# Decay broadcasts on the GpSimd queue, and the first FFN block's input products inside the last SSD step

## The chip, the cores and the metric

The kernel runs on one core of one Trainium2 chip. The metric is the device time of one execution in microseconds (us). The engines are called as in the profile: PE is TensorE (PEld its weight loads), DVE is VectorE, ACT is ScalarE, POOL is GpSimd, SP is SyncE. SPq and POOLq are the DMA issues of SP and POOL.

## The reference

One inference step of a two-layer trunk over 1024 prompt tokens and 8 samples of 8 tokens, width 1024, in float32. Layer 0 has an SSD mixer, layer 1 an S5 mixer, and each mixer is followed by a SwiGLU FFN:

```python
for i in range(DEPTH):
    sh1, sc1, g1, sh2, sc2, g2 = split(silu_c @ ada_w[i] + ada_b[i], 6)
    h = rms(x) * (1 + sc1) + sh1
    out = ssd_mixer(h) if i % 2 == 0 else s5_mixer(h)
    x = x + g1 * out
    h = rms(x) * (1 + sc2) + sh2
    x = x + g2 * swiglu(h)
```

The SSD mixer projects h to z, x, B, C and dt, runs a short convolution and silu over x, B and C, and then a chunked scan. Within a chunk of 128 tokens, with a_cs the running sum of dt * A for each head:

```python
decay = exp(where(causal, a_cs[l] - a_cs[s], -inf))
y_diag = einsum(C B^T * decay, x * dt)
y_off = einsum(C, state_in) * exp(a_cs)
```

The result is gated with silu(z), normed over each of 8 groups, and projected back.

## The kernel before

The tokens are in two halves of the class Half: 512 prompt tokens, and 512 with the 64 sample tokens behind them. Features lie on partitions and tokens along the free dimension. Every weight and activation of a dense product is split into two float32r parts, and a product takes three matmuls (`mm3`, lines 134 to 136). A weight comes in by one 512 KB load from SP (`weight_cols`, `weight_block`, lines 122 and 129), is cast on ScalarE (line 114) and its remainder is taken on VectorE (line 115). Loads of ada_w (line 327) are slipped in ahead of weight loads as long as any are left. There are three buffers for loaded weights and two for split ones.

`mixers` runs 16 steps, one for each half and each of the 8 groups. A step consists of `ssd` for its group, `z_part`, the `out_proj` that is due (groups in the parts 0, 1-2, 3-4, 5-6, 7), `group_out`, and `begin` for the next step, which holds the input products and convolutions. At the last group of a half `begin` also makes the z products and the norm factors of the other half. A 17th round of the loop held only the last `out_proj`.

In `ssd` a chunk needs two things that are spread over partitions out of DRAM. `decays` (line 554) loads ab, the running sums of four heads, to every partition, 128 x 4 x 128 values, 256 KB; ScalarE makes exp(a[l] - a[s]) of it (lines 556 and 558), VectorE masks it (line 598), and PE takes it at line 605 (py). ab has three buffers. Line 579 loads ea, exp(a_cs), in two transfers for a chunk, 64 KB each, into two buffers. In the second half a fifth chunk holds the samples; `sample_state` loads and stores their states from SP.

The group norm of `group_out` takes the squares' sum over 256 features (`rstd_cols`, small products gp and gb, and Newton steps on VectorE) and gives pairs yh, yl, four buffers each, to `out_proj`. `ffn_norm` (through `norm`, `modulated`, lines 214, 220, 240, 241) gives the pairs h of the FFN. `ffn_in` makes some tiles of the hidden features, two weight matrices for each; `ffns` runs `ffn_in` one block ahead of `out_proj`. During FFN tiles `side` takes one or two steps of `s5_matrices`, the preparation of the S5 layer, whose POOL transfers are lines 995, 1007, 1023, 1035 and 1039; the S5 layer's own input transfers are lines 1079 and 1082.

What sets the order: the program is traced in the order of the code, which gives each instruction its priority, and a planner with a cost model then lays out each engine's queue and the buffers' use at compile time. An engine, and a DMA queue, works its list in that order; waits are semaphores.

Of the kernel before, what the change touches and what calls it, by code (L numbers as in the profile page):

```python
# [6 lines left out]
F32 = mybir.dt.float32  # L7
# [28 lines left out]
class Half:  # L36
    """A part of the tokens: 512 of the prompt, the second one with the samples behind them."""
# [13 lines left out]
class Trunk:  # L51
    def __init__(self, tc, ctx, ins, outs):
# [4 lines left out]
        self.pn = None  # L57
# [25 lines left out]
    def mixc(self, shape, name):  # L83
        """A constant of the mixers alone."""
        return self.cm.tile(shape, F32, name=name, tag=name)
# [39 lines left out]
    def weight_block(self, w, r0, nk, c0, n):  # L125
        """Rows r0.. (nk tiles) and columns c0.. of a weight matrix."""
# [23 lines left out]
    def add_resid(self, hf, li, piece, ft, o, n, src):  # L150
        """x += gate * src for the columns o.. of a half."""
# [13 lines left out]
    def rstd_cols(self, tiles, hf, scale, eps, name):  # L165
        """1/sqrt(mean of squares over the partitions of all tiles + eps): a column for each 128 tokens."""
# [8 lines left out]
        # by token on partitions: 1/sqrt from a first guess out of the exponent, in three Newton steps  # L175
# [18 lines left out]
    def rstd(self, tiles, hf, scale, eps, name):  # L194
        """The same along the tokens, on every partition."""
# [12 lines left out]
    def modulated(self, hf, li, sh, sc, ft, r, out, pview, sview):  # L208
        """out = x * r * (1 + scale) + shift; the views arrange the columns of out."""
# [21 lines left out]
    def norm(self, hf, li, sh, sc, r=None):  # L231
        """The modulated norm of x as float32r pairs, a pair for each 128 features."""
# [13 lines left out]
    def constants(self):  # L246
# [6 lines left out]
        # causal[s, l] = 1 where l >= s  # L253
# [3 lines left out]
        # bmask[s, b] = 1 where token s is of sample b  # L257
# [7 lines left out]
        # two[j, p] = 1 where p // 64 == j  # L265
# [5 lines left out]
    def flip(self, src, rows, name, alloc=None):  # L271
        """Rows of 128 values (a DRAM view [rows, 128]) as columns: [128, rows]."""
# [9 lines left out]
    def load_x(self, hf):  # L282
        """A function for each 128 tokens of a half."""
# [39 lines left out]
    def ada(self, li, cb, j):  # L323
        """Rows j * 256.. of silu(c) @ ada_w for 512 columns, 128 columns in each quarter of the partitions."""
# [16 lines left out]
    def ada_out(self):  # L341
        """The last such product + ada_b (+ 1 for the scales), as columns of mod."""
# [14 lines left out]
    def ssd_setup(self):  # L357
# [19 lines left out]
        # sblk[s, l] = 1 where s and l are tokens of one sample; pick[s, b] = 1 for the first token of b  # L377
# [5 lines left out]
        # conv states of the samples, [128, tile, (b, k)]  # L383
# [6 lines left out]
    def conv_states(self):  # L390
        """A function for each quarter of the samples' conv states."""
# [15 lines left out]
    def dt_part(self, hf, h):  # L407
        """dt, its running sums and decays, by head on partitions and by token on partitions."""
# [26 lines left out]
        # softplus: max(v, 0) + log(1 + e^-|v|), the logarithm by the series of atanh  # L435
# [15 lines left out]
        # running sums over the tokens of a chunk, and the whole sums  # L451
# [26 lines left out]
        # by head on partitions, to spread over the partitions from DRAM  # L478
# [13 lines left out]
    def conv_tile(self, hf, h, c0, t, pad):  # L492
        """A tile of x, B or C: in_proj, conv and silu. t: its index in the conv's channels."""
# [56 lines left out]
    def decays(self, col, m, g, acs):  # L550
        """exp(a[l] - a[s]) for the four heads of a group, [s, head, l]; 1 where l < s."""
        nc = self.nc
        ab = self.mp.tile([P, 4, P], F32, name=self.nm("ab"), tag="ab", bufs=3)
        nc.sync.dma_start(ab[:m, :, :m], self.d_acs[None, 4 * g : 4 * g + 4, col : col + m].broadcast_to([m, 4, m]))
# [6 lines left out]
    def ssd(self, hf, g, tok, C, B, xt, y):  # L561
# [7 lines left out]
        for c in range(nck + (1 if hf.samples else 0)):  # L569
# [6 lines left out]
            if not first:  # L576
                ea = self.mp.tile([P, 2, P], F32, name=self.nm("ea"), tag="ea")
                for j in range(2):
                    nc.sync.dma_start(
# [59 lines left out]
    def sample_state(self, g, C, xe, bt, yv, ea):  # L639
        """The samples' part of y that comes from their states, and their new states."""  # L640
# [40 lines left out]

    def group_out(self, hf, g, y, xt, zs):
        """The gated group norm of y, as pairs for out_proj."""
# [7 lines left out]
        for t in range(2):  # L691
            u = y[:, t]
            V.scalar_tensor_tensor(u, u, self.nw[:, 2 * g + t : 2 * g + t + 1], r, MUL, MUL)
            yh = self.mp.tile([P, hf.n], F32R, name=self.nm("yh"), tag="yh", bufs=4)
            yl = self.mp.tile([P, hf.n], F32R, name=self.nm("yl"), tag="yl", bufs=4)
# [5 lines left out]
    def mixers(self):  # L701
        """The SSD layer over both halves."""
# [17 lines left out]
        for i in range(len(steps) + 1):  # L720
            if i < len(steps):
                hf, g = steps[i]
                C, B, xt = nxt
                y = self.mp.tile([P, 2, hf.n], F32, name=self.nm("y"), tag="y", bufs=1)
                self.ssd(hf, g, tok, C, B, xt, y)
                if g < GR - 1:
                    zs = self.z_part(hf, h, g)
                else:
                    zs = z
                    if hf.i == 0:  # L730
                        h = self.norm(self.halves[1], 0, 0, 1, r)
                    else:
                        self.ahead = self.ffn_norm(0, self.halves[0], r)
            if due:
                self.out_proj(due[0], 0, 2, self.ssd_out_w[0], 2 * due[1] * P, due[2])
                due = None
            if i < len(steps):
                done += self.group_out(hf, g, y, xt, zs)
                for p in parts:
                    if p[-1] == g:  # L740
                        due = (hf, p[0], done)
                        done = []
            if i + 1 < len(steps):
                nxt = begin(i + 1)

    def out_proj(self, hf, li, piece, w, r0, yp):
        """x += gate * (pairs yp) @ (rows r0.. of w)."""
# [35 lines left out]
    def ffn_in(self, li, hf, c0, nt):  # L783
        """Some tiles of the hidden features, as pairs."""
        nc = self.nc
        if c0 == 0:
# [5 lines left out]
        for j in range(nt):  # L792
# [3 lines left out]
            u = self.fp.tile([P, hf.n], F32, name=self.nm("fu"), tag="fu", bufs=2)  # L796
# [5 lines left out]
            yh = self.fp.tile([P, hf.n], F32R, name=self.nm("fh"), tag="fh")  # L802
            yl = self.fp.tile([P, hf.n], F32R, name=self.nm("fl"), tag="fl")
# [9 lines left out]
    def ffns(self, steps, more=(), last=()):  # L813
        """FFN steps; more: what else to emit behind a step; last: what to emit ahead of the last part's product."""
# [13 lines left out]
    def cmul(self, ore, oim, ar, ai, br, bi, t1, t2):  # L828
        """(ore, oim) = a * b, complex; the outputs are not among the inputs."""
# [8 lines left out]
    def s5_matrices(self):  # L838
# [7 lines left out]
        with self.tc.tile_pool(name="s5pre", bufs=1) as pp, self.tc.tile_pool(name="s5big", bufs=1) as bp:  # L846
# [15 lines left out]
            # ang - 2 pi round(ang / 2 pi), the multiple of 2 pi in three parts  # L862
# [8 lines left out]
            # sine and cosine of half the angle by their series  # L871
# [11 lines left out]
            # sin = 2 a b, cos = 1 - 2 a a  # L883
# [7 lines left out]
            # q = (a - 1) / lambda  # L891
# [14 lines left out]
            # to [(j n), q]  # L906
# [6 lines left out]
            # powers 0..8 of a  # L913
# [19 lines left out]
            # Bbar [(j n), q, i]  # L933
# [9 lines left out]
            # C_re and -C_im as [(j n), q, i]  # L943
# [14 lines left out]
            # the same with the two groups of a pair in columns of their own  # L958
# [9 lines left out]
            # D in the last 16 of 128 rows, for the diagonal of lag 0  # L968
# [14 lines left out]
            def powers(q0):  # L983
# [9 lines left out]
                # Or = Re(C a^(l+1)), Oi = -Im(C a^(l+1))  # L993
# [348 lines left out]
```

## Time and profile before

| | us |
|---|---|
| median of 3 runs | 3255.96 |
| lowest and highest run | 3253.51, 3258.48 |
| span of the profiled execution | 3254.6 |
| PE busy in it | 3094.3 |
| DVE, ACT, POOL busy in it | 1903.7, 1222.6, 175.5 |

The span runs from the first to the last instruction of one execution on the chip; the profile gives no further time around it. The mixers end near 1250 us, the first FFN of layer 0 follows. The page names the engine's busy time, the queries of the trace give single instructions with the idle time ahead of them and what ended it. "PEclk" is the clock granted to PE as a share of full speed.

### The profile page before, as it was taken

The page shows a single profiled execution, that of the slowest core. Times are in us where ns is not written, and L with a number is a line of the kernel's source. Part 1 is how long each engine was busy: PE and PEld are TensorE (multiplying, and loading weights), DVE is VectorE, ACT ScalarE, POOL GpSimd, SP SyncE. Part 2 cuts the span into 40 slices and gives each one's busy share as a digit, 9 for nine tenths or more (in the row PEclk, how much of TensorE's full clock was granted, in tenths as well). Part 3 has the DMA queues.
Part 4 walks back from the last instruction along what each step waited for, and adds up shares of the span by engine and source line. Part 5 has one row for each costly group of instructions (what it writes and reads, how often), then busy time and mean ns, then how long its engine had stood idle before and what let it go on. Part 6 is the DMA issues. An engine that isn't in the chain of part 4 may idle for free.

```text
span 3254.6 us, 52528 instructions
## 1 busy us (share of the span) xinstructions
PE 3094.3 (95%) x20800; PEld 2719.9 (84%) x20800; DVE 1903.7 (58%) x4269; ACT 1222.6 (38%) x2183; POOL 175.5 (5%) x360
## 2 busy tenths in 40 slices
PE   7999999999999998999999989999998999999998
PEld 5777777788888986777899989988877879999998
DVE  4776668666677677865464572446448243544344
ACT  4553445444444444222342224235332442422222
POOL 0010000111011100102001000000000000000000
PEclk7999999999999998999999999999999999999999
DMA  6445554545434333444433436333452642223221
GB/s 224 141 134 179 154 163 123 156 138 146 120 95 124 102 90 84 122 129 131 126 96 123 154 104 195 99 96 99 135 166 80 207 130 78 80 84 110 78 89 65
DMA packets 552057, 402.74 MB, mean 124 GB/s; under 512 B 50323, under 2 KB 501291, under 8 KB 551796
## 3 DMA queue, kind: packets, MB, share of 16 engines
q1 hardware_dynamic: 545156, 377.36, 39.1%
q0 software_dynamic: 6656, 22.03, 2.3%
q8 instruction: 164, 2.69, 0.3%
q14 instruction: 81, 0.66, 0.1%
HBM read 363.70 MB, written 46.89 MB: 126 GB/s over the span
## 4 chain that ended last, share of the span: by engine, by line
PE 70%; DVE 10%; DMA 9%; issue 7%; ACT 3%; POOL 1%; SPq 0%; ACTq 0%; POOLq 0%; DVEq 0%
PE mm L134 15%; PE mm L136 15%; PE mm L135 15%; PE mo L134 5%; PE mo L136 5%; PE mo L135 5%; DMA ab<-d_acs 4%; DMA om<-d_o 2%; DVE wl L115 2%; DMA aw<-in_ada_w_dram 2%; PE ada L334 1%; PE py L605 1%; PE y L1156 1%; PE sn L674 1%; DVE sc L1115 1%
## 5 line engine op out<-in xcount | busy, mean ns | idle before, releaser
L136 PE MATMUL mm<-hh,wl 128*128 128x288 f32 (+3 forms) x3672 | 1213.1, 330 | 15.9 <-DVE wl L115 15.8
L134 PE MATMUL mm<-hh,wh 128*128 128x288 f32 (+3 forms) x3672 | 1218.8, 332 | 7.4 <-ACT wh L114 2.4
L135 PE MATMUL mm<-hl,wh 128*128 128x288 f32 (+3 forms) x3672 | 1211.3, 330 | 0.0
L114 ACT CAST wh<-wr 128x1024 fp32r<-128x1024 f32 (+1 forms) x426 | 445.6, 1047 | 1140.9 <-PE mm L135 762.2
L136 PEld LDWEIGHTS mm<-hh,wl 128*128 128x128 f32 (+1 forms) x3672 | 693.7, 189 | 71.1 <-DVE wl L115 22.2
L134 PEld LDWEIGHTS mm<-hh,wh 128*128 128x128 f32 (+1 forms) x3672 | 693.7, 189 | 69.6 <-issue 10.0
L115 DVE TENSOR_TENSOR wl<-wr,wh 128x1024 fp32r<-128x1024 f32 (+1 forms) x426 | 519.1, 1219 | 386.9 <-ACT wh L114 374.9
L135 PEld LDWEIGHTS mm<-hl,wh 128*128 128x128 f32 (+1 forms) x3672 | 693.9, 189 | 53.0 <-issue 5.3
L134 PE MATMUL mo<-fh,wh 128*128 128x288 f32 (+1 forms) x1056 | 351.2, 333 | 16.2 <-DVE x L156 10.2
L156 DVE SCALAR_TENSOR_TENSOR x<-mo,mod,x 128x288 f32<-128x288 f32 (+2 forms) x408 | 231.7, 570 | 210.7 <-PE mo L136 210.1
L136 PE MATMUL mo<-fh,wl 128*128 128x288 f32 (+1 forms) x1056 | 348.8, 330 | 4.0 <-DVE wl L115 4.0
L135 PE MATMUL mo<-fl,wh 128*128 128x288 f32 (+1 forms) x1056 | 347.8, 329 | 0.0
L801 DVE TENSOR_TENSOR fu<-fu,mm 128x288 f32<-128x288 f32 (+1 forms) x132 | 70.0, 531 | 312.7 <-PE mm L136 311.3
L134 PEld LDWEIGHTS mo<-fh,wh 128*128 128x128 f32 x1056 | 200.3, 190 | 35.5 <-issue 10.9
L136 PEld LDWEIGHTS mo<-fh,wl 128*128 128x128 f32 x1056 | 200.2, 190 | 19.6 <-DVE wl L115 4.9
L135 PEld LDWEIGHTS mo<-fl,wh 128*128 128x128 f32 x1056 | 200.5, 190 | 14.0
L522 DVE SCALAR_TENSOR_TENSOR xbc<-pre,cw,xbc 128x512 f32<-128x512 f32 (+1 forms) x288 | 161.6, 592 | 11.5 <-ACT xbc L508 9.3
L556 ACT ACTIVATE ab<-ab,tacs 128x128 f32<-128x128 f32 (+1 forms) x288 | 97.0, 390 | 133.0 <-DMA ab<-d_acs 115.3
L134 PE MATMUL mo<-yh,wh 128*128 128x288 f32 (+1 forms) x384 | 133.5, 348 | 9.5 <-DVE rs L160 4.9
L135 PE MATMUL mo<-yl,wh 128*128 128x288 f32 (+1 forms) x384 | 129.8, 338 | 0.0
L136 PE MATMUL mo<-yh,wl 128*128 128x288 f32 (+1 forms) x384 | 128.9, 337 | 0.3 <-DVE wl L115 0.3
L134 PEld LDWEIGHTS mo<-yh,wh 128*128 128x128 f32 x384 | 74.2, 194 | 22.9 <-issue 8.7
(368 smaller groups left out, 3232.8 us busy)
## 6 DMA issues: line engine op xcount, KB each, us to landing
wr<-in_ffn_w_in_dram SPq DMA_DIRECT2D x176, 512.0 KB
aw<-in_ada_w_dram SPq DMA_DIRECT2D x96, 512.0 KB
wr<-in_ssd_in_w_dram SPq DMA_DIRECT2D x96, 512.0 KB
wr<-in_ffn_w_out_dram SPq DMA_DIRECT2D x88, 512.0 KB
ab<-d_acs SPq DMA_DIRECT2D x64, 256.0 KB
wr<-in_ssd_out_w_dram SPq DMA_DIRECT2D x32, 512.0 KB
wr<-in_s_glu_w_dram SPq DMA_DIRECT2D x32, 512.0 KB
st<-in_state_ssm_dram SPq DMA_DIRECT2D x32, 256.0 KB
```

Source lines behind the costliest of these rows:

```text
L114: nc.scalar.copy(hi, raw)
L115: nc.vector.tensor_tensor(lo, raw, hi.bitcast(F32), SUB)
L134: mm(ps, wh, hh, start=first, stop=False)
L135: mm(ps, wh, hl, start=False, stop=False)
L136: self.last_mm = mm(ps, wl, hh, start=False, stop=last)
L156: nc.vector.scalar_tensor_tensor(self.xs(hf, ft, o, npr), src[:, :npr], mod[:, t, 0:1], self.xs(hf, ft, o, npr), MUL, ADD)
L334: nc.tensor.matmul(self.ada_ps[q * 32 : (q + 1) * 32], self.ct[:, 2 * j + k, :], w[:, k, q * P : (q + 1) * P], start=j + k == 0, stop=j == ...
L522: V.scalar_tensor_tensor(dst, src(k), w(k), dst, MUL, ADD)
L556: nc.scalar.activation(ab[:m, r, :m], ab[:m, r, :m], AF.Relu, bias=acs[:m, 4 * g + r : 4 * g + r + 1], scale=-1.0)
L605: nc.tensor.matmul(py[q * HD : (q + 1) * HD, (r // 2) * P : (r // 2) * P + m], xd[:m, r * HD : (r + 1) * HD], w[:m, r, :m], start=True, st ...
L674: nc.tensor.matmul(pn[q], xe[r, t * P : (t + 1) * P], bb[r].rearrange("p b k -> p (b k)"), start=True, stop=True)
L801: nc.vector.tensor_tensor(u[:, o : o + n], u[:, o : o + n], pu[:, :n], MUL)
```

## The change

`decays` and the ea loads are issued by POOL in place of SP. `mixers` loses its 17th round: in the last step `ssd_finish` (the output of the convolution states) and the FFN norm of the first half are traced ahead of `ssd`, the first FFN block's `ffn_in` (two tiles) between the due `out_proj` and `group_out`, and the last `out_proj` and the block's own `out_proj` follow the loop. For that block the hidden pairs come out of the buffers of yh and yl, and the product u out of the pool for temporaries. `ffns` starts with the second block. Comments and docstrings are gone, which moves no instruction.

```diff
@@ decays, ssd
-        nc.sync.dma_start(ab[:m, :, :m], self.d_acs[None, 4 * g : 4 * g + 4, col : col + m].broadcast_to([m, 4, m]))
+        nc.gpsimd.dma_start(ab[:m, :, :m], self.d_acs[None, 4 * g : 4 * g + 4, col : col + m].broadcast_to([m, 4, m]))
...
-                    nc.sync.dma_start(
+                    nc.gpsimd.dma_start(
                         ea[j * HD : (j + 1) * HD, :, :m],
@@ group_out
+    def ypair(self, hf):
+        return tuple(self.mp.tile([P, hf.n], F32R, name=self.nm(t), tag=t, bufs=4) for t in ("yh", "yl"))
@@ mixers
-        for i in range(len(steps) + 1):
...
+        ffn = self.ffn_steps(0, self.halves[0])[0]
+        for i in range(len(steps)):
+            hf, g = steps[i]
+            end = i + 1 == len(steps)
+            C, B, xt = nxt
+            y = self.mp.tile([P, 2, hf.n], F32, name=self.nm("y"), tag="y", bufs=1)
+            if end:
+                self.ssd_finish()
+                self.ahead = self.ffn_norm(0, self.halves[0], r)
+            self.ssd(hf, g, tok, C, B, xt, y)
+            if g < GR - 1:
+                zs = self.z_part(hf, h, g)
+            else:
+                zs = z
+                if not end:
+                    h = self.norm(self.halves[1], 0, 0, 1, r)
             if due:
                 self.out_proj(due[0], 0, 2, self.ssd_out_w[0], 2 * due[1] * P, due[2])
                 due = None
...
+            if end:
+                hid = self.ffn_in(*ffn)
+            done += self.group_out(hf, g, y, xt, zs)
...
+            if not end:
                 nxt = begin(i + 1)
+        self.out_proj(due[0], 0, 2, self.ssd_out_w[0], 2 * due[1] * P, due[2])
+        self.out_proj(ffn[1], 0, 5, self.ffn_w_out[0], 0, hid)
@@ ffn_in
+        early = self.fp is None
...
+            u = (self.th([P, hf.n], "fu") if early else
+                 self.fp.tile([P, hf.n], F32, name=self.nm("fu"), tag="fu", bufs=2))
...
+            if early:
+                yh, yl = self.ypair(hf)
@@ front, run
             self.mixers()
-            self.ssd_finish()
...
-            fa, fb = self.ffn_steps(0, A), self.ffn_steps(0, B)
+            fa, fb = self.ffn_steps(0, A)[1:], self.ffn_steps(0, B)
...
-                more = [[], [], [], [], [], [s5_a]]
+                more = [[], [], [], [], [s5_a]]
```

## Rows read from the trace of the kernel before

**Rows 1.** The page's first part: busy us of each engine, share of the span, instructions.

```profile
PE 3094.3 (95%) x20800; PEld 2719.9 (84%) x20800; DVE 1903.7 (58%) x4269; ACT 1222.6 (38%) x2183; POOL 175.5 (5%) x360
```

**Rows 2.** Busy time in two wide stretches: the stretch and its length, then busy us of PE, PEld, DVE, ACT and POOL (with instructions), the granted clock, the DMA share and GB/s.

```profile
80.00:1200.00 1120.00, 1071.40 (x7791) 892.97 (x7790) 789.64 (x1724) 522.51 (x1141) 113.36 (x251) 0.98 0.47 134
1200.00:1250.00 50.00, 35.60 (x223) 28.27 (x223) 35.67 (x90) 21.38 (x41) 1.20 (x1) 0.76 0.25 71
```

**Rows 3.** Who waited for whom: us in total, times, longest; ACT and PE from 80 to 1200 us, SP over the whole span.

```profile
ACT ab L556 <- DMA ab<-d_acs: 115.3, 48, 6.9
...
PE py L605 <- DVE ab L598: 24.2, 19, 2.3
...
SPq L122 <- DVE wl L115: 1062.5, 210, 16.2
```

**Rows 4.** PE's instructions in order of time around the end of the mixers: start, duration, line, operation, tiles, shapes, and in brackets the idle time ahead with what ended it.

```profile
1223.79 0.37 PE L134 MATMUL mo<-yh,wh 128*128 128x288 f32 x1 [1.89 <-DVE rs L160]
...
1235.50 2.30 PE L181 MATMUL gp<-ones_d,gq 128*128 128x1 f32 x10 [9.66 <-DVE gq L173]
1240.13 2.39 PE L203 MATMUL gb<-ident,gy 128*128 128x128 f32 x10 [2.33 <-DVE gy L191]
...
1242.89 1.29 PE L771 MATMUL cop<-ident,cst 128*120 128x128 f32 x4
1244.55 0.85 PE L134 MATMUL mo<-yh,wh 128*128 128x288 f32 x2 [0.37 <-ACT yh L696]
...
1248.89 0.40 PE L136 MATMUL mo<-yh,wl 128*128 128x288 f32 x1
```

**Rows 5.** Busy time in short stretches, columns as in Rows 2: three at the end of the mixers, one in the S5 preparation.

```profile
1220.00:1230.00 10.00, 3.95 (x27) 3.40 (x25) 10.00 (x24) 7.11 (x11) 0.00 (x0) 0.76 0.24 67
1230.00:1240.00 10.00, 2.30 (x10) 2.21 (x10) 7.27 (x20) 3.13 (x5) 0.00 (x0) 0.50 0.18 52
1240.00:1250.00 10.00, 9.35 (x39) 7.98 (x40) 4.67 (x10) 3.97 (x11) 0.00 (x0) 0.54 0.09 24
...
1450.00:1500.00 50.00, 50.00 (x246) 41.91 (x245) 34.40 (x74) 12.98 (x19) 3.78 (x7) 1.00 0.39 127
```

**Rows 6.** DVE's instructions in order of time at the end of the last SSD step.

```profile
1220.46 0.28 DVE L617 TENSOR_TENSOR y<-y,py 128x128 f32<-128x128 f32 x1
1220.66 1.29 DVE L241 TENSOR_TENSOR hl<-mt,hh 128x512 fp32r<-128x512 f32 x2
...
1223.07 0.45 DVE L156 SCALAR_TENSOR_TENSOR x<-mo,mod,x 128x224 f32<-128x224 f32 x1
1223.43 0.21 DVE L160 TENSOR_TENSOR rs<-mo,mod 128x64 f32<-128x64 f32 x1
...
1224.12 0.81 DVE L687 SCALAR_TENSOR_TENSOR y<-xbc,dsk,y 128x576 f32<-128x576 f32 x1
...
1232.36 1.22 DVE L115 TENSOR_TENSOR wl<-wr,wh 128x1024 fp32r<-128x1024 f32 x1
```

**Rows 7.** PE's instructions in order of time ahead of the last SSD step.

```profile
1152.89 1.17 PE L181 MATMUL gp<-ones_d,gq 128*128 128x1 f32 x10
...
1160.42 1.30 PE L203 MATMUL gb<-ident,gy 128*128 128x128 f32 x10
...
1177.38 0.49 PE L585 MATMUL pt<-ident,xbc 128*128 128x128 f32 x3
```

**Rows 8.** PE's instructions in order of time in the first FFN block.

```profile
1262.86 0.40 PE L136 MATMUL mm<-hh,wl 128*128 128x512 f32 x1
1263.10 0.39 PE L134 MATMUL mm<-hh,wh 128*128 128x512 f32 x1
```

**Rows 9.** SP's DMA issues in order of time: start and the time that the issues took.

```profile
608.83 0.37 SPq L327 DMA_DIRECT2D aw<-in_ada_w_dram  x1
609.99 0.37 SPq L554 DMA_DIRECT2D ab<-d_acs  x1
...
1243.13 11.24 SPq L774 DMA_DIRECT2D out_dram<-co  x8
```

**Rows 10.** POOL's instructions in order of time: two state products of the last SSD step, and the first transfer of the S5 layer.

```profile
1182.19 0.61 POOL L626 TENSOR_TENSOR S<-S,decb 128x256 f32<-128x256 f32 x1 [24.69 <-PE py L614]
1189.17 1.43 POOL L626 TENSOR_TENSOR S<-S,decb 128x256 f32<-128x256 f32 x1 [6.37 <-PE py L614]
...
1703.78 0.57 POOL L1079 DMA_DIRECT2D d_h<-u  x1 [156.22 <-ACT u L220]
```

**Rows 11.** The chain of work that ended last, in order of time: start, duration, what.

```profile
609.99 5.11 DMA ab<-d_acs
...
1032.63 3.26 DMA ab<-d_acs
```

**Rows 12.** DMA issues by line: queue, count, KB each, median us from issue to landing.

```profile
d_o<-ot POOLq DMA_DIRECT2D x16, 256.0 KB, 2.5
d_v<-vt POOLq DMA_DIRECT2D x16, 256.0 KB, 3.5
...
d_u<-d_h POOLq DMA_DIRECT2D x8, 288.0 KB, 7.3
```

**Rows 13.** POOL's groups by line over the span: busy us, mean ns of one, idle us before with what ended it.

```profile
L1082 POOL DMA_DIRECT2D d_u<-d_h x16 | 12.2, 799 | 6.9 <-issue 4.5 <-DMA d_h<-u 2.4
...
L995 POOL DMA_DIRECT2D d_o<-ot x16 | 8.7, 546 | 82.4 <-DVE ot L836 64.6 <-DVE kt L1020 9.3 <-DVE nt L190 8.2
```

More of the change, by code (lines that the diff above doesn't have):

```diff
@@ L56, in __init__ @@
         self.uid = 0
-        self.pn = None
+        self.pn = self.fp = None
         self.ada_prev = self.ahead = None
@@ L693, in group_out @@
             V.scalar_tensor_tensor(u, u, self.nw[:, 2 * g + t : 2 * g + t + 1], r, MUL, MUL)
-            yh = self.mp.tile([P, hf.n], F32R, name=self.nm("yh"), tag="yh", bufs=4)
-            yl = self.mp.tile([P, hf.n], F32R, name=self.nm("yl"), tag="yl", bufs=4)
+            yh, yl = self.ypair(hf)
             nc.scalar.copy(yh, u)
@@ L719, in mixers @@
         done, due, nxt = [], None, begin(0)
-        for i in range(len(steps) + 1):
[L721 to L733, printed above, removed]
+        ffn = self.ffn_steps(0, self.halves[0])[0]
[14 more added lines that the diff above has]
+                    h = self.norm(self.halves[1], 0, 0, 1, r)
             if due:
@@ L736, in mixers @@
                 due = None
[L737 to L743, printed above, removed]
+            if end:
+                hid = self.ffn_in(*ffn)
+            done += self.group_out(hf, g, y, xt, zs)
+            for p in parts:
+                if p[-1] == g:
+                    due = (hf, p[0], done)
+                    done = []
+            if not end:
                 nxt = begin(i + 1)
+        self.out_proj(due[0], 0, 2, self.ssd_out_w[0], 2 * due[1] * P, due[2])
+        self.out_proj(ffn[1], 0, 5, self.ffn_w_out[0], 0, hid)
     def out_proj(self, hf, li, piece, w, r0, yp):
@@ L795, in ffn_in @@
             wu = self.weight_cols(w_in, DFF + m * P)
-            u = self.fp.tile([P, hf.n], F32, name=self.nm("fu"), tag="fu", bufs=2)
+            u = (self.th([P, hf.n], "fu") if early else
+                 self.fp.tile([P, hf.n], F32, name=self.nm("fu"), tag="fu", bufs=2))
             for o, n in hf.blocks:
@@ L801, in ffn_in @@
                 nc.vector.tensor_tensor(u[:, o : o + n], u[:, o : o + n], pu[:, :n], MUL)
-            yh = self.fp.tile([P, hf.n], F32R, name=self.nm("fh"), tag="fh")
-            yl = self.fp.tile([P, hf.n], F32R, name=self.nm("fl"), tag="fl")
+            if early:
+                yh, yl = self.ypair(hf)
+            else:
+                yh = self.fp.tile([P, hf.n], F32R, name=self.nm("fh"), tag="fh")
+                yl = self.fp.tile([P, hf.n], F32R, name=self.nm("fl"), tag="fl")
             a = nc.scalar.copy(yh, u)
```

## The prediction

> **What bounds the kernel now.** I read the page first for each engine's share, then wide stretches for where the matmul engine PE stands still, then the waits of PE and of the engines ahead of it, and only then single instructions. PE is busy for 3094.3 of 3254.6 us [rows 1]. The change moves arithmetic and removes none, so it can win only idle time of PE, 160.3 us in all, and what PE loses where its clock falls. All that it touches lies ahead of 1262 us, and there the idle time has two shapes: from 80 to 1200 us it is 48.6 us out of 1120, in crumbs; from 1200 to 1250 us alone it is 14.4 us, at a granted clock of 0.76 [rows 2]. The two halves of the change answer to the two.
>
> The crumbs: their largest single cause is PE waiting for the masked decays, 24.2 us in 19 waits; behind it stands ScalarE, which waits 115.3 us in 48 waits for the transfers into ab [rows 3]. A wait of ScalarE is not yet one of PE: dense products cover most of them.
>
> The hole: the reader is to follow PE from 1221 to 1249 us. It waits 1.89, 9.66, 2.33 and 0.37 us, with the group norm's small products between [rows 4]. VectorE is full from 1220 to 1230 us [rows 5], and half of what it does is the FFN norm of the first half (L241, and L214 in pairs of the same length), which stands between the last y and the group norm's own operations (L687) [rows 6]. So the hole is the chain of the last group norm, made longer by the FFN norm, with no dense product left beside it.
>
> **The tail, step by step.** I sum against the profiled span, 3254.6 us; the median of the runs, 3255.96, is 1.4 us above it, and I put that back at the end.
>
> What can be had: 1.89 + 9.66 + 2.33 + 0.37 = 14.25 us of idle time, and the clock. It was granted at 0.76, 0.50 and 0.54 in the three slices [rows 5]: after the idle stretch PE runs at the lower of its two levels, 1.2 GHz. The ten products gp take 2.30 us there against 1.17 at full clock, the gb 2.39 against 1.30 [rows 4, 7], so what takes twice as long costs half: out_proj's products from 1244.55 to 1248.89 us lose 2.2 us. Together 1.13 + 1.09 + 2.2 = 4.4 us, and the ceiling of this half is 18.6 us.
>
> What fills it: the first FFN block, 2 tiles x 2 matrices x 8 features x 3 products = 96 products of 512 columns, each 0.24 us behind the last [rows 8]: 23 us of dense work for a hole of 14 to 19 us. In the new order it needs only the FFN norm and four weight pairs.
>
> What moves with it. (1) The FFN norm goes ahead of the last SSD step: 16 operations of about 0.6 us on VectorE, 9.7 us [rows 6]. Its outputs take the buffers of the second half's h, free when z is through, at 1177 us, where the step's first products pt start [rows 7]. From there it holds the step's first chunks back by about 5 us. What hides that is out_proj, 8 tiles x 2 blocks x 4 pairs x 3 = 192 products of 288 columns, by width 0.135 us each, 26 us; without that cover it would cost the 5 us. (2) ssd_finish goes ahead of the step too. Four of its transposes take 1.29 us [rows 4], so eight some 2.6 us, there or here. Its eight output transfers kept SP from 1243.13 to 1254.37 us [rows 9]; now they stand in front of state and weight transfers whose buffers are mostly not free yet. I take nothing, and up to 4 us if they are late. (3) The group norm, freed of the FFN norm but beside four weight splits of 1.22 us [rows 6], should last 12 to 14 us instead of the 24 from the last y to out_proj [rows 4, 6]. If the step ends near 1225 us, out_proj of the last part can start at 1237 to 1239 us, and PE has dense work until 1177 + 43 (what it does now up to 1220) + 2.6 + 23 = 1246 us. So the last out_proj starts where it did, at full clock, with 23 us of FFN work behind it; less the 2.6 us of transposes and some 2 us of new stalls, and never more than the ceiling. (4) The two out_proj calls stand back to back: 12 products, 1.6 us for a feature tile, against 2 x (0.45 + 0.21) = 1.3 us of additions on VectorE [rows 6]. The margin is thin: 0 to 3 us. (5) The S5 side steps are called three times less in the first half: 33 calls before, 32 of them needed; now 30, and three more in the next block, still ahead of the S5 layer. POOL idles for 156 us between the last of their work and that layer's input [rows 10], so the delay is hidden. The sum: 18.6 less about 2 is **-17 us**, bounds -19 and -8.
>
> **The broadcasts.** 72 ab (one a chunk) and 128 ea (two a chunk, but for the first chunk of a group in the first half) leave SP for POOL. What SP gains is worth nothing by itself: its long waits are for a weight buffer, 1062.5 us in 210 waits [rows 3], so weights are issued as soon as there is room. What counts is when an ab lands. On SP, two of the critical ones take 5.11 and 3.26 us from issue until ScalarE starts [rows 11]; the longer one stands 1.2 us behind a 512 KB ada load on the same queue [rows 9], the shorter comes after the ada loads have ended. POOL loads nothing of this shape in the trace. From below: its 256 KB stores land in 2.5 and 3.5 us; from above: d_u, 288 KB in short pieces from DRAM to DRAM, in 7.3 us [rows 12]. An ab is 256 KB in 512-byte rows, nearer to the stores in size and without d_u's detour, and on POOL's queue no weight load is ahead of it. I take 3.5 us, 0.5 to 1 us sooner than now; ends: 2 us sooner, 3 us later.
>
> What queues behind it: a POOL issue costs 0.55 to 0.8 us [rows 13], so a chunk's three cost about 1.9 us beside a state product of 0.61 us, in chunks 7 us apart [rows 10]. The 200 issues add some 120 us to an engine busy for 175.5 of 3254.6 us [rows 1]. An ab for chunk c + 3 waits for the decays of chunk c, the state product for the products behind them, so both come free nearly together; a conv copy that waits for ScalarE can stand ahead only of the next group's ab, which has time in hand. An ab that is 0.5 to 1 us sooner takes that off each of the 19 exposed waits, 9 to 19 us at most; but the planner lays out a new static order, which moves crumbs both ways. I take **-5 us**, bounds -20 and +55 (19 waits x 2.9 us).
>
> One thing speaks against this half. POOL's state product takes 0.61 us, and 1.43 us where VectorE is busy beside it [rows 10]; yet its DMA issues of d_o keep to a mean of 546 ns [rows 13] in a stage with VectorE busy for 34.4 of 50 us [rows 5]. The Trainium skill (SBUF — State Buffer, section "SBUF: two separate sides") says in its box on the trap of VectorE blocking DMA that a DMA issued from GpSimd cannot write its descriptors while VectorE holds their shared port, and gives about 620 ns alone against 3100 ns. By that figure 19 exposed waits would cost 47 us and the estimate would be 3286 us; the row of the issues disagrees, that of the state products agrees.
>
> **The rivals.** (A, slower) The ab land later from POOL. The price is 19 to 48 waits times the delay; against the tail's 17 us it decides from 17 / 48 = 0.35 us to 17 / 19 = 0.9 us. With 1.5 us on 24 waits: 3255.96 - 17 + 36 = 3275 us; with 2.9 us on 19: 3294. For it: d_u's 7.3 us and 512 short rows for each ab. Against: the stores. (A2) VectorE holds POOL up in the issue itself, as it does the state product: 0.82 us on 19 to 48 waits is 16 to 39 us, 3255.96 - 17 + 27 = 3266 us. Against: the 546 ns. The page above describes this one. (B) The change does not do what it says: the planner, which took VectorE for faster than it is when it placed the weight split now found at 1232.36 us [rows 6], puts the FFN products where they leave the hole open. Then only the FFN norm's 9.7 us leave the chain, less some stalls: -8 us, 3248 us. (C) Both halves give all: 3255.96 - 19 - 20 = 3217 us.
>
> **How the numbers follow.** Forecast 3255.96 - 17 - 5 = **3234 us** with 0.62, own range 3222 to 3246. B has 0.15, A 0.14, A2 0.04, C 0.05. The range 3217 to 3262 leaves out nearly all of A and A2 and a little below, under 0.2. A measurement of this kernel can tell about 0.2%, 6.5 us, from no change. Faster by more: 0.62 + 0.05 + half of B, 0.75 rounded; within: the other half of B and mild cases of A, 0.10; slower: 0.15.
>
> **What would show it.** In the new profile the stretch from the last z product to out_proj of the last part should hold 96 products of 512 columns at clock 1.00, with no wait of PE for the group norm over 2 us. PE's waits for the decays should be at or under 24.2 us and ScalarE's for ab under 115.3. If they have grown, A is right, and the place is the issue on POOL or the landing behind it. What would make the prediction wrong is an ab issue that takes POOL well over 0.8 us, or one that stands behind a copy waiting for ScalarE.

## The result, and the profile after

The changed kernel takes 3282.3 us (median; 3267.7 to 3291.4) against 3256.5 us of the kernel before on the same chip: a ratio of 1.0069 (95% interval 1.0045 to 1.0092). It is slower by 0.7%, 26 us, where the forecast was 3234 us, 22 us faster. The profiled execution is one of the shorter ones, with a span of 3272.2 us, 17.6 us over that of before [rows 1].

The page's first part, after:

```profile
PE 3109.4 (95%) x20800; PEld 2727.2 (83%) x20800; DVE 1906.9 (58%) x4267; ACT 1222.8 (37%) x2185; POOL 300.1 (9%) x560
```

Against [rows 1] PE is busy for 15 us more with the same 20800 instructions, and idle for 162.8 us, only 2.6 us more than before. POOL has the 200 issues more that the change gives it, and 125 us of work more, as forecast.

Where the time goes is read from two pairs of marks that both programs have: the first operation of the group norm of the 15th step, and the multiplication that ends the 30th FFN tile, each before and after (VectorE's instructions in order of time; start, duration, line, operation):

```profile
1144.90 1.55 DVE L687 SCALAR_TENSOR_TENSOR y<-xbc,dsk,y 128x576 f32<-128x576 f32 x2
...
1722.66 0.45 DVE L801 TENSOR_TENSOR fu<-fu,mm 128x288 f32<-128x288 f32 x1 [1.09 <-PE mm L136]
```

```profile
1172.62 1.54 DVE L690 SCALAR_TENSOR_TENSOR y<-xbc,dsk,y 128x576 f32<-128x576 f32 x2
...
1743.91 0.46 DVE L810 TENSOR_TENSOR fu<-fu,mm 128x288 f32<-128x288 f32 x1 [1.09 <-PE mm L136]
```

At the first mark, where of the whole change only the broadcasts have acted, the kernel is 27.7 us late. From there to the second, across the new order of the last step, it wins 6.5 us back (27.7 to 21.2). So the broadcasts cost about 28 us in this execution, and the tail won about 6, not 17 (from the second mark to the end another 3.6 us go, which neither half explains).

What the waits say of the first part (total, times, longest; 80 to 1200 us, after):

```profile
POOL ab L554 <- PE py L605: 247.2, 41, 18.4
...
ACT ab L556 <- DMA ab<-d_acs: 105.3, 53, 8.2
...
PE py L605 <- DVE ab L598: 15.6, 13, 4.0
```

Against [rows 3] there is no rise to be seen: ScalarE's waits for ab fell from 115.3 to 105.3 us (113.9 us in 55 waits over the whole span, since the changed kernel still has chunks behind 1200 us), PE's waits for the masked decays from 24.2 to 15.6. The prediction's own test ("PE's waits for the decays should be at or under 24.2 us", ScalarE's under 115.3) is passed, with the kernel 28 us late. The lateness shows in the sums of the stretch instead (columns as in [rows 2]):

```profile
80.00:1200.00 1120.00, 1059.96 (x7589) 879.00 (x7588) 774.38 (x1672) 515.05 (x1123) 232.10 (x440) 0.97 0.47 132
```

PE is idle for 60.0 us in place of 48.6 there, and the granted clock is 0.97 in place of 0.98, which over 1120 us is some 11 us (an estimate from two rounded rows). The planner had laid out another order, so that no single wait carries the cost. The experiments had to take this apart.

And the second part, PE in order of time at the end of the mixers, after:

```profile
1281.72 1.17 PE L181 MATMUL gp<-ones_d,gq 128*128 128x1 f32 x10
1286.95 2.36 PE L203 MATMUL gb<-ident,gy 128*128 128x128 f32 x10 [4.06 <-DVE gy L191]
1291.33 0.85 PE L134 MATMUL mo<-yh,wh 128*128 128x288 f32 x2 [2.02 <-ACT yh L698]
```

VectorE in the same stretch, after:

```profile
1263.13 0.82 DVE L690 SCALAR_TENSOR_TENSOR y<-xbc,dsk,y 128x576 f32<-128x576 f32 x1
...
1269.86 0.76 DVE L173 TENSOR_TENSOR gq<-gq,gq 128x576 f32<-128x576 f32 x1 [0.75 <-ACT gq L171]
```

The squares gq are ready at 1270.6 us, but their sum gp runs on PE at 1281.72, without a wait of its own: for those 11 us PE works through the FFN products, which stand ahead of gp in its queue (some 20 of the 96 had run inside the step, the other 76 directly before gp). Then the norm is late, with nothing left beside it, and PE waits 4.06 and 2.02 us, where it was 14.25 us in all before [rows 4], at the lower clock again: gb takes 2.36 us, as in [rows 4], against 1.30 at full clock [rows 7].

### The profile page after: what moved, and what is told of

The parts are those of the page before. It is cut to its first block, busy times and chain, and to the rows that moved or that the text cites. A ratio compares the mean times of both kernels' runs of the same rounds, so it can differ in the third digit from the quotient of the medians.

```text
span 3272.2 us, 52604 instructions
## 1 busy us (share of the span) xinstructions
PE 3109.4 (95%) x20800; PEld 2727.2 (83%) x20800; DVE 1906.9 (58%) x4267; ACT 1222.8 (37%) x2185; POOL 300.1 (9%) x560
## 4 chain that ended last, share of the span: by engine, by line
PE 66%; DVE 10%; DMA 10%; issue 8%; ACT 4%; POOL 1%; SPq 0%; ACTq 0%; POOLq 0%; DVEq 0%
PE mm L134 14%; PE mm L136 14%; PE mm L135 14%; DMA ab<-d_acs 5%; PE mo L134 5%; PE mo L136 5%; PE mo L135 4%; DVE wl L115 2%; DMA om<-d_o 2%; DMA aw<-in_ada_w_dram 1%; PE ada L334 1%; PE y L1168 1%; PE sn L674 1%; PE py L605 1%; ACT ab L556 1%
## 5 line engine op out<-in xcount | busy, mean ns | idle before, releaser
L134 PE MATMUL mo<-fh,wh 128*128 128x288 f32 (+1 forms) x1040 | 344.0, 331 | 16.0 <-DVE x L156 10.0
L135 PE MATMUL mo<-fl,wh 128*128 128x288 f32 (+1 forms) x1040 | 340.9, 328 | 0.0
L134 PE MATMUL mo<-yh,wh 128*128 128x288 f32 (+1 forms) x400 | 141.6, 354 | 14.5 <-DVE rs L160 5.3
L556 ACT ACTIVATE ab<-ab,tacs 128x128 f32<-128x128 f32 (+1 forms) x288 | 95.1, 388 | 120.8 <-DMA ab<-d_acs 113.9
L136 PE MATMUL mo<-yh,wl 128*128 128x288 f32 (+1 forms) x400 | 135.5, 340 | 0.5 <-DVE wl L115 0.5
```

Of the source, the lines that this page charges most:

```text
L134: mm(ps, wh, hh, start=first, stop=False)
L135: mm(ps, wh, hl, start=False, stop=False)
L136: self.last_mm = mm(ps, wl, hh, start=False, stop=last)
L556: nc.scalar.activation(ab[:m, r, :m], ab[:m, r, :m], AF.Relu, bias=acs[:m, 4 * g + r : 4 * g + r + 1], scale=-1.0)
```

## The experiments

Each time stands beside runs of the kernel before on the same chip.

### Which half costs, and which transfer

e1_bcast is the kernel before with both broadcasts on POOL, e3_ab with ab alone, e4_ea with ea alone. e2_tail is the changed kernel with both back on SP.

```diff
@@ decays (e1_bcast, e3_ab)
-        nc.sync.dma_start(ab[:m, :, :m], ...)
+        nc.gpsimd.dma_start(ab[:m, :, :m], ...)
@@ ssd (e1_bcast, e4_ea)
-                    nc.sync.dma_start(
+                    nc.gpsimd.dma_start(
                         ea[j * HD : (j + 1) * HD, :, :m],
```

> The kernel before with the ab and ea transfers on POOL, and nothing else of the change. Theory T (the broadcasts cost more than the tail wins): 3256 + 28 = 3284 us, range 3274 to 3294, since by the end of the 15th SSD step the changed kernel ran 28 us behind. The prediction's own step (-5 us) says 3251. Rival R1 (the new order of the last step upset the planner's whole layout, the broadcasts are harmless): 3256, within 0.2%. ScalarE's waits for ab should grow in number or length by T.

> The changed kernel with the ab and ea transfers back on SP: the last step's new order alone. The prediction's step says 3256 - 17 = 3239 us (3237 to 3248). From the shifts of the two traces (the changed kernel lost 28 us up to the end of step 15, regained 15 by the 12th output tile, lost 9 of them again in the FFN that follows) I expect 3247 to 3249. Rival R1 (the tail's order costs and the broadcasts do not) says 3270 to 3285.

> The kernel before with only ab moved to POOL, ea left on SP. T1 (ab itself lands later from POOL, now that SP's weight loads run beside it instead of behind it): nearly all of the cost, 3276 to 3286 us. T2 (POOL's queue is crowded by 200 issues and what stands before them; ea has 128 of them): half or less, 3262 to 3270.

> The kernel before with only ea moved to POOL, ab left on SP. T1: ea is off the path and SP is freed for ab, so 3250 to 3258 us. T2: POOL's issues of ea hold the state products up, which make the next chunk late: 3262 to 3272.

| kernel | us | before, us | ratio (95%) |
|---|---|---|---|
| e1_bcast | 3286.3 | 3259.5 | 1.0095 (1.0077 to 1.0113) |
| e2_tail | 3251.2 | 3259.5 | 0.9986 (0.9971 to 1.0000) |
| e3_ab | 3290.2 | 3259.5 | 1.0106 (1.0087 to 1.0126) |
| e4_ea | 3262.0 | 3259.5 | 1.0010 (0.9995 to 1.0025) |

The halves add up: +0.95% and -0.14% make +0.81%, within the interval of the change itself. The cost is ab's; the 128 issues of ea cost 2.5 us, which cannot be told from nothing, and at most 8 by the interval. So POOL's queue is not simply crowded by the number of its issues. What e1_bcast expected of ScalarE's waits for ab did not come: 111.4 us in 56 waits over the span. The tail brings 5 to 8 us, with an interval that just reaches no change. Its trace agrees: the two marks stand at

```profile
1137.90 1.55 DVE L690 SCALAR_TENSOR_TENSOR y<-xbc,dsk,y 128x576 f32<-128x576 f32 x2
...
1710.60 0.46 DVE L810 TENSOR_TENSOR fu<-fu,mm 128x288 f32<-128x288 f32 x1 [1.09 <-PE mm L136]
```

which is 5.1 us less from one to the other than before. That this execution is 7 us early at the first mark, ahead of all that the tail changes, says how far the planner's order and a single execution can shift a profile.

### The planner's order, or the chip

Moving one transfer makes the planner lay out every queue anew. e10_pool_oldorder is e3_ab with the queues of PE, ScalarE and VectorE pinned to the order that the kernel before has (places stored as a list; POOL and SP stay free); e11_sp_neworder is the mirror, ab on SP in the order of e3_ab.

```diff
+def pin(tc):
...
+    for engine, packed in QUEUES.items():
+        mine = [i for i in traced if i.engine == getattr(mybir.EngineType, engine)]
...
+            tc.add_manual_dep(
+                mine[at], last.name,
+                mybir.DependencyInfo(mybir.DependencyClass.NoSync, mybir.DependencyReason.DATA), reason="pin")
+            last = mine[at]
```

> The kernel of e3_ab (ab on POOL, +30 us) with the queues of PE, ScalarE and VectorE pinned, instruction by instruction, to the order that the kernel before has; only POOL's and SP's queues differ from before. Theory H (the chip: an ab from POOL is there 0.6 to 0.8 us later, whatever the order): the cost stays or grows, since the old order expects the ab earlier, 3280 to 3300 us. Theory P (the planner: it laid the other three queues out anew for an ab from POOL, and that order costs): the cost goes, 3255 to 3265 us.

> The mirror of it: the kernel before, ab on SP, with the queues of PE, ScalarE and VectorE pinned to the order of e3_ab. Theory H: 3255 to 3262 us, as before. Theory P: as e3_ab, 3280 to 3292 us. Something between would share the 30 us out between the two.

e10_pool_oldorder: 3307.9 against 3258.6 us, 1.0167 (1.0149 to 1.0186). e11_sp_neworder: 3259.4 against 3258.6, 1.0004 (0.9995 to 1.0014). Theory H holds: the order made for POOL costs nothing by itself, and in the old order ab on POOL costs 49 us, more than the 3300 us at which H's range ended. Against e3_ab, the planner's new order hid some 19 of them.

With PE's order the same to the instruction, the traces can be laid side by side. One chunk, in the kernel before: the last products that read an ab buffer, the next issue into it, ScalarE's first operation on it.

```profile
394.13 0.66 PE L605 MATMUL py<-ab,xd 128*64 128x128 f32 x8
...
394.83 0.37 SPq L554 DMA_DIRECT2D ab<-d_acs  x1
...
398.11 0.99 ACT L556 ACTIVATE ab<-ab,tacs 128x128 f32<-128x128 f32 x3 [0.45 <-DMA ab<-d_acs]
```

The same chunk in e10_pool_oldorder, and below it POOL's group of these issues over the span (busy us, mean ns of one) and the wait of ScalarE from 80 to 1200 us:

```profile
406.25 0.66 PE L605 MATMUL py<-ab,xd 128*64 128x128 f32 x8
...
407.22 0.75 POOL L554 DMA_DIRECT2D ab<-d_acs  x1 [3.40 <-PE py L605]
...
411.36 0.99 ACT L556 ACTIVATE ab<-ab,tacs 128x128 f32<-128x128 f32 x3 [0.84 <-DMA ab<-d_acs]
```

```profile
L554 POOL DMA_DIRECT2D ab<-d_acs x72 | 55.0, 764 | 525.8 <-PE py L605 406.1 <-PE mo L136 24.1 <-DVE wl L115 20.8
```

```profile
ACT ab L556 <- DMA ab<-d_acs: 150.8, 53, 7.3
...
PE py L605 <- DVE ab L598: 37.3, 23, 4.0
```

From the buffer's release (394.79 and 406.91 us) SP begins the issue 0.04 us later, POOL 0.31 us; the issue takes 0.37 and 0.75 us; ScalarE starts 3.32 and 4.45 us after the release. This is one chunk. Over the 51 chunks in which ScalarE stood idle ahead of its first operation on ab in both traces, the mean from release to that operation is 4.08 us before and 4.87 here: 0.78 us later. Its waits are 35 us longer than in [rows 3], 45.5 us over the whole span (160.8 us in 55 waits), which is nearly the whole cost. PE's idle time rises from 160.3 us [rows 1] to 201.0 us, 3299.1 less 3098.1 busy. Of these 41 us only 13 are at py in this stretch and 15 over the span; the rest is at other products, the samples' sy and the transposes pt among them.

### Is it POOL's own path, or the loads that SP no longer holds back?

On SP an ab that waits for its buffer holds up the weight loads behind it; from POOL it does not, and the loads can run beside it. A first pair of runs left one row of each ab on SP (e12_hold), or put one row on POOL (e13_one_row), with SP's queue pinned too.

```diff
+        src = self.d_acs[None, 4 * g : 4 * g + 4, col : col + m]
+        nc.sync.dma_start(ab[:1, :, :m], src)
+        nc.gpsimd.dma_start(ab[1:m, :, :m], src.broadcast_to([m - 1, 4, m]))
```

> The kernel of e10_pool_oldorder (ab on POOL, +49 us) with the first of the 128 rows of each ab left on SP and the other 127 on POOL, and SP's queue pinned too, to the order of the kernel before. So SP waits at the same places as before and issues each weight load no sooner than before. Theory W (the loads that SP no longer holds back run beside ab and make it late): the cost goes, 3258 to 3272 us. Theory Q (the path from POOL itself is longer: a later start of the issue, a longer issue, a later landing): it stays, 3295 to 3315 us.

> The same the other way round: 127 rows of each ab on SP as before, one row of 2 KB on POOL, all four queues pinned as in e12_hold. If the price of POOL's path is one for each transfer whatever its size (theory Q1), this costs as much as e10_pool_oldorder, 3290 to 3310 us; if it is one of the size, of the 512 short pieces that POOL has to describe (theory Q2), it costs little, 3256 to 3270 us.

4220.8 us, 1.2958 (1.2929 to 1.2988), and 4050.1 us, 1.2437 (1.2415 to 1.2459): neither theory. The page of e12_hold, POOL's issues, and its DMA issues (KB each, median us from issue to landing):

```profile
L556 POOL DMA_DIRECT2D ab<-d_acs x72 | 299.2, 4156 | 925.8 <-PE py L607 687.2
...
ab<-d_acs POOLq DMA_DIRECT2D x64, 254.0 KB, 21.0
```

A piece of 127 rows takes 4.16 us to issue and 21.0 us to land, where 128 rows take 0.76 and 4.4. So these two runs say nothing on the question. It was put again with pieces of 32 and 96 rows: e14_hold32 (32 on SP, 96 on POOL), e15_pool32 (32 on POOL, 96 on SP), and the control e16_sp_split (both on SP, SP's queue free).

> As e12_hold, with a split that avoids 127 rows: the first 32 rows of each ab on SP, the other 96 on POOL, the queues of PE, ScalarE, VectorE and SP pinned to the order of the kernel before. Theory W (the loads that SP no longer holds back make ab late): SP's order is back, so the cost goes, 3256 to 3270 us. Theory Q (POOL's path is longer in itself): most of the 49 us of e10_pool_oldorder stay, 3285 to 3310 us.

> The other way round: the first 32 rows on POOL, 96 on SP, same pins. Theory W: 3256 to 3270 us. Theory Q1 (the price of POOL's path is one for each transfer): 3285 to 3310 us, as e14_hold32. Theory Q2 (it goes with the size, four times as many pieces to describe): 3258 to 3275 us, well under e14_hold32.

> The control: the same 32 and 96 rows, both issued by SP, PE, ScalarE and VectorE pinned to the order of before. If the split itself costs nothing: 3255 to 3264 us. One more issue of 0.4 us on SP ahead of the last piece may cost up to 20 us.

3275.3 us, 1.0049 (1.0031 to 1.0066); 3260.6, 1.0006 (0.9993 to 1.0019); 3272.3, 1.0040 (1.0027 to 1.0053), each against 3259.3. The control spoils the first: the split alone costs 13 us. The second misses Q1's number and meets Q2's, but POOL's piece of 32 rows lands in 3.6 us (median) and need not be the last of the two, so it does not decide between them. The last run moves the whole ab and holds SP with a wait in place of a transfer (HELD lists the transfers that stood behind an ab on SP, each with the number k of its chunk; pys are the products that end the reading of each ab):

```diff
+            for at, k in HELD:
+                tc.add_manual_dep(
+                    mine[at], pys[k - 3].name,
+                    mybir.DependencyInfo(mybir.DependencyClass.Sync, mybir.DependencyReason.DATA), reason="held")
```

> The kernel of e10_pool_oldorder (whole ab on POOL, PE, ScalarE and VectorE in the order of before, +49 us) with SP pinned to the order of before as well, and with the transfer that stood behind an ab on SP waiting for the same products that free ab's buffer, so that SP issues no load sooner than it did before. Theory W (the loads made ab late): the cost falls to 20 us or less, 3258 to 3278 us, and the extra time from release to ScalarE falls from 0.78 to under 0.4 us. Theory Q (POOL's path): 3295 to 3315 us, 0.7 to 0.85 us.

3303.1 against 3258.5 us, 1.0149 (1.0125 to 1.0173). Theory Q's time holds, with a delay just under its range. In the trace SP issues its other transfers in the order of before, and none that stood behind an ab before that ab's release. With SP holding its loads back, 45 of the 49 us stay, and the extra time from release to ScalarE is 0.66 us (53 chunks, 4.10 to 4.76). All of it lies in the issue: on these chunks it begins 0.29 us later (0.11 to 0.40) and takes 0.37 us longer (0.40 to 0.77), and what follows it takes 3.60 and 3.59 us. The competing loads are left with the 0.1 us between 0.78 and 0.66; the 5 us between the two times lie inside the intervals.

One more rival is on POOL itself: an ab that waits there holds up the state products behind it. In e10_pool_oldorder VectorE waits 16.7 us for them in place of 8.4. But in e15_pool32 it waits 13.6 us, at a cost of 1.3 us in all, so this is not where the time goes.

All runs with PE's, ScalarE's and VectorE's order held fixed, by their mean extra time from release to ScalarE (from the profiled executions) and their cost (medians, against the kernel before):

| kernel | extra, us a chunk | cost, us | cost / extra |
|---|---|---|---|
| e11_sp_neworder | -0.03 | 0.8 | |
| e15_pool32 | 0.05 | 1.3 | |
| e14_hold32 | 0.23 | 15.9 | 69 |
| e16_sp_split | 0.24 | 13.0 | 54 |
| e17_wait | 0.66 | 44.5 | 67 |
| e10_pool_oldorder | 0.78 | 49.3 | 63 |

(e11's order is that of e3_ab.) The cost goes with the lateness, whatever made it, at 54 to 69 us for each us, as if 54 to 69 of the 72 chunks passed it on; which chunks do was not followed. The costs of e14_hold32 and e16_sp_split have wide intervals (10 to 22 and 9 to 17 us). In the planner's own order the price is lower: e1_bcast, 0.66 us later over 49 chunks, costs 27 us, 41 for each us.

### Can the lateness be hidden, and does less of it help?

e5_after_ab4 gives the changed kernel a fourth ab buffer, e6_tail_ab4 the same to e2_tail; e9_split is the kernel before with ab in three pieces by heads on SP.

```diff
-        ab = self.mp.tile([P, 4, P], F32, name=self.nm("ab"), tag="ab", bufs=3)
+        ab = self.mp.tile([P, 4, P], F32, name=self.nm("ab"), tag="ab", bufs=4)
...
-            cb = self.mp.tile([P, P], F32, name=self.nm("cbm"), tag="cbm")
+            cb = self.mp.tile([P, P], F32, name=self.nm("cbm"), tag="cbm", bufs=1)
@@ e9_split
-        nc.sync.dma_start(ab[:m, :, :m], ...)
+        for a, b in ((2, 4), (1, 2), (0, 1)):
+            nc.sync.dma_start(ab[:m, a:b, :m], self.d_acs[None, 4 * g + a : 4 * g + b, col : col + m].broadcast_to([m, b - a, m]))
```

> The changed kernel with four ab buffers in place of three (the masked C B product, which only VectorE writes and reads, goes down to one buffer to make room). Theory L (the 0.6 to 0.8 us that pass in addition between an ab buffer coming free and ScalarE starting on it are the whole cost, because three buffers close a loop over that time): a fourth buffer lets the transfer start a chunk earlier, so nearly all of the 28 us come back, 3250 to 3262 us. Rival W (the weight loads that no longer stand behind the broadcasts on SP delay them and other work): the transfers still run beside them, 3272 to 3285 us.

> The kernel of e2_tail (broadcasts on SP, new order of the last step) with four ab buffers and one masked C B buffer. Theory L: the loop over the landing of ab costs the kernel before as well (24 us of PE waits in 19 of them), so 10 to 25 us come off: 3226 to 3242 us. Rival W: the landing is covered by dense work on the whole, 3245 to 3255 us.

> The kernel before with each ab transfer split in three on SP (heads 2 and 3, then head 1, then head 0, which ScalarE takes first): the last piece is issued some 0.8 us later, and nothing goes to POOL. It prices latency alone, with SP's order kept. Theory L: ScalarE starts 0.4 to 0.8 us later after each release, and that costs 15 to 30 us as it does from POOL, 3271 to 3290 us. Rival W: the order on SP is kept, so little changes, 3255 to 3263 us.

e5_after_ab4: 3269.9 against 3258.0 us, 1.0034 (1.0022 to 1.0047). e6_tail_ab4: 3251.8, 0.9983 (0.9971 to 0.9996), no better than e2_tail. e9_split: 3258.7, 1.0002 (0.9988 to 1.0017). A fourth buffer brings the change from 25.8 us over the kernel before to 11.9, and brings nothing on SP. Theory L's numbers fail in both, W's hold in e6_tail_ab4 alone. With the tail's gain taken out (each against the tail alone with as many buffers) the broadcasts cost 0.51% with four buffers and 0.83% with three: the loop over the release is part of it, not the whole. What the rest is with four buffers stays open, since the planner's order changed there too. e9_split did not price what it was meant to: ScalarE can begin on the first head that is there, and its waits became 93 shorter ones in place of 48.

### The rest of the hole

e7_swap is e2_tail with two statements exchanged:

```diff
-            if end:
-                hid = self.ffn_in(*ffn)
             done += self.group_out(hf, g, y, xt, zs)
+            if end:
+                hid = self.ffn_in(*ffn)
```

> The kernel of e2_tail with the last group norm traced ahead of the first FFN block's input products instead of behind them. In e2_tail the squares were ready at 1236.9 us, but the sum over them stood on PE behind all 96 FFN products and ran at 1248.6 us, and PE then waited 4.0 and 2.0 us. Theory O (the order on PE's queue, not the length of the norm, left the rest of the hole): these 6 to 7 us of waits go, 3242 to 3247 us. Rival V (VectorE is the bound, and the norm's operations ahead of the weight splits make the FFN products wait instead): 3249 to 3256 us.

3243.7 against 3258.0 us, 0.9955 (0.9939 to 0.9970): 14 us, and theory O holds. PE at the end of the mixers in e7_swap:

```profile
1242.30 1.25 PE L181 MATMUL gp<-ones_d,gq 128*128 128x1 f32 x10
1247.71 1.30 PE L203 MATMUL gb<-ident,gy 128*128 128x128 f32 x10 [0.18 <-DVE gy L191]
1256.20 0.30 PE L134 MATMUL mo<-yh,wh 128*128 128x288 f32 x1
```

VectorE there:

```profile
1235.92 1.55 DVE L690 SCALAR_TENSOR_TENSOR y<-xbc,dsk,y 128x576 f32<-128x576 f32 x2
...
1241.40 0.76 DVE L173 TENSOR_TENSOR gq<-gq,gq 128x576 f32<-128x576 f32 x1 [1.46 <-ACT gq L171]
```

gp now follows the squares at once (1242.16 to 1242.30), FFN products stand between gp, gb and out_proj, gb runs at full clock (1.30 us), and PE waits 0.18 us for the norm where the changed kernel had 4.06 and 2.02. What is left are waits of 1.26, 0.19 and 0.84 us in out_proj for VectorE's additions, inside the 0 to 3 us of the prediction's step (4). Between the two marks this execution is 19 us shorter than before (1147.14 to 1705.49). This kernel, with the broadcasts on SP, is faster than both the kernel before and the changed one.

## Why the prediction was wrong, point by point

- **What bounds the kernel** held for PE and for the hole, which could be filled (e7_swap). Its sentence on ScalarE's waits did not hold; see the third point.
- **"I take 3.5 us, 0.5 to 1 us sooner than now"** is the step that failed. ab lands 4.3 us after its issue in the changed kernel, and ScalarE starts 4.86 us after the release in place of 4.13 (48 chunks): 0.73 us later. On these chunks the issue begins 0.32 us later (0.08 to 0.40) and takes 0.38 us longer (0.38 to 0.76); what follows it takes as long as from SP, 3.67 and 3.70 us. So the transfer itself is not slower from POOL and not quicker either: from issue to ScalarE it is 4.46 us in the mean, 4.05 from SP, where 3.5 had been taken, and to be off the queue of the weight loads wins nothing that shows. The stores of [rows 12] were the wrong neighbours. Most of what was needed stood in the rows: an issue on SP of 0.37 us [rows 9], one on POOL of 0.55 to 0.80 us [rows 13]. The prediction counted this as time of an idle engine; it is on the path of every ab that waits for its buffer. The Trainium skill (DMA: Bandwidth & Descriptors, section "Specifications") gives about 1 us to the first byte from GpSimd and 0.6 from SP. By it the delay would be 0.4 us, an estimate; the traces show 0.66 to 0.78, in the same direction.
- **"19 exposed waits"** was the second error. ScalarE waits in 48 to 53 chunks and works its queue in order, so what stands behind an ab is late as well: 41 us for each us of delay in the planner's order and 54 to 69 with the order held, not 19. "A wait of ScalarE is not yet one of PE" is true for a wait that the order was laid out for, not for a longer one.
- **"Bounds -20 and +55"** held for the term, +27 us measured (e1_bcast), but by two errors against each other: the upper end took a delay of 2.9 us on 19 waits.
- **What queues behind an issue on POOL** held. In e10_pool_oldorder 66 of 69 issues start within 2 us of the release, and ea, with more issues, costs nothing that can be told (e4_ea).
- **The tail, -17 us,** came to -5 to -8 (e2_tail). The step that failed is (3), "the last out_proj starts where it did, with 23 us of FFN work behind it". The 96 products stood ahead of the norm's sum on PE's queue, not beside it. From the first operation of the norm to out_proj it was 28.2 us (1263.13 to 1291.33), against a forecast of 12 to 14 for the norm. In e7_swap, with the norm ahead in the code, these are still 20.3 us (1235.92 to 1256.20), but covered; and -14 us come. Of the 18.6 us in sight, the changed kernel leaves 6.1 as waits and, by [rows 4, 7], about 3.3 to the lower clock at gb and out_proj.
- **Moved with it:** new stalls of PE, 1.30 us at the moved output transposes and 1.47, 0.37 and 1.60 us at out_proj, are 4.7 us where 2 were allowed. With the 6.1 and 3.3 us they leave some 4.5 of the 18.6, close to the gain measured. The late S5 steps cost nothing by the 30th FFN tile.
- **Rivals.** A came in its mechanism, with under half the delay of its example (0.66 us for 1.5) and a price of 41 us for each us in place of 24. B came too, for its result (-8 us), though by the order of the code and not by a slow weight split. 3256 + 27 - 8 = 3275 us against 3282 measured, whose interval begins at 3271. A2 did not: the 72 issues in the changed kernel take 754 ns in the mean and 0.97 us at the longest; the 10 with VectorE busy for under a fifth of them take 727 ns, the 17 with it busy for over four fifths 771 ns. The 3100 ns that the Trainium skill gives (SBUF — State Buffer, section "SBUF: two separate sides") do not show here. Nor is "busy beside it" what lengthened the state product: VectorE worked beside the one of 0.61 us as well. In that trace 8 of the 56 products take over 0.7 us, each beside a weight split, an FFN-norm or a convolution operation of VectorE, and none of the other 48 runs beside a weight split.

## What to carry to other kernels

A transfer that waits for its buffer has the issue itself on its path: compare what two queues need from the release to the landing before moving it, and price the difference by every wait of the in-order engine behind it, not only by the waits that reach the bounding engine. Work meant to stand beside a chain must be queued behind the chain's own small products, or it stands in front of them. When a planner rearranges all queues, a fall in the waits that one watches proves nothing (ScalarE's for ab fell while the kernel lost 26 us); pin the order, and the same trace can be read line against line.

## What the runs showed of the hardware that was not expected

A broadcast load into 127 partitions from POOL took 4.16 us to issue and 21.0 us to land (e12_hold), one into 128 partitions 0.76 and 4.4 us (e10_pool_oldorder), one into 96 rows 0.68 and 3.8 us (e14_hold32). From SP it is nearly as bad: in e13_one_row, with 127 rows from SP, ScalarE waited 835 us for ab, against 115.3 before, while the single row from POOL landed in 4.8 us (median). The Trainium skill (DMA: Bandwidth & Descriptors, section "Why a DMA increments its semaphore by 16 and not by 1") says that a transfer is spread over the largest number of engines, up to 16, that divides its slowest dimension, and gives 127 partitions as a case for one engine. It names an exception on trn2 for some copies from GpSimd. The times agree with the rule and not with the exception, though no row here shows the engines themselves.

The issue of a broadcast load holds POOL for a time that hardly shrinks with its size: 0.56 us in the mean for one row (e13_one_row), 0.57 for 32 (e15_pool32), 0.68 for 96 (e14_hold32), 0.76 for 128 (e10_pool_oldorder), against 0.41 for 128 rows on SP (before).
